# A two-layer GDN and FoX trunk: the opening in two column halves, kept PSUM banks, the last gates in other buffers, and other planned distances

## The chip, the cores and the metric

The kernel runs on one NeuronCore of a Trainium2 chip, in one launch. The metric is the device time of one execution in microseconds (us). The kernel before was timed three times: 1981.58 us in the median, 1981.22 to 1984.26. One further execution was profiled; spans and waits below come from it. In the profile PE is TensorE, PEld its weight loads, DVE is VectorE, ACT ScalarE, POOL GpSimd and SP SyncE, which issues nearly all DMA transfers.

## The reference

The trunk has two layers over 1024 tokens of width 1024 in float32, steered by one vector c:

```python
cond = jax.nn.silu(c)
for i in range(DEPTH):
    mod = cond @ ada_w[i] + ada_b[i]
    shift, scale, gate = jnp.split(mod[:, None, :], 3, axis=-1)
    h = rmsnorm(x, norm_w[i]) * (1 + scale) + shift
    y = gdn_mixer(...) if i % 2 == 0 else fox_mixer(...)
    x = x + gate * y
return rmsnorm(x, final_norm_w)
```

Layer 0 is a gated delta rule (GDN): h times the input projection gives q and k for 8 heads and v and z for 16 heads of 128, and two gates per v head (b and a). q, k and v pass through a causal convolution of width 4 and SiLU. In chunks of 64 tokens (the kernel takes 128) the rule is

```python
T = inverse of (I + L),  L = strictly lower part of (k*beta) k^T * decay
v_new = T @ (v*beta) - (T @ (k*beta*exp(g))) @ state
o     = (q*exp(g)) @ state + attn @ v_new
state = state * exp(g_last) + k_dec^T @ v_new
```

The output is normed per head, multiplied by silu(z) and projected by a 2048 x 1024 matrix. Layer 1 is attention with a forget gate (FoX), 16 heads of 64. The change concerns layer 0 and the way to layer 1 alone.

## The kernel before

**Stages.** Layer 0 works on two halves of 512 tokens (h = 0, 1), and in each on eight groups g: one q/k head with its two v heads. The opening (`start_norm`, L547) norms and transposes the first half of x, builds shift and scale (`scol`, `gcol`) from `ada_w`, modulates to `ht_h` and `ht_l` (each float32 value split into two parts) and projects the gates. `proj_all` (L801) then runs through 16 groups: k, q, two v tiles and two z tiles each. A tile is 8 k steps of `mm3`, three 128x128 by 128x512 matmuls (high by high, high by low, low by high), so 24 matmuls; 96 tiles make 2304 of them. Beside that flow run `prepk`, `invert_blocks`, `invert_merge` (the inverse T, by blocks, with a round trip through DRAM), `prepv` and `prep2` (transposes to token order, attention products), `chain` (the state recurrence) and `finish` (norm, gate, store of `og_d` and `ogl_d`). `out_proj_a` (L460) multiplies by the output matrix, half 0 with `ohi`, `olo` and half 1 with `yh`, `yl`, loaded back from `og_d` and `ogl_d`; the results go through POOL (L506) and are stored to `x_d` (L508) for layer 1.

**What sets the order.** A small planner in Python (`Flow`, L89) writes TensorE's program. Each stream is a generator with a priority; it issues matmuls and yields a number of nanoseconds before which it isn't to be taken up again. The planner's clock `flow.t` advances by a cost per matmul, so that a yield of 1700 means some eight wide matmuls of other streams in between. The `Y_*` constants are these distances. `bank`, `both` and `free` (L145 to L165) plan PSUM banks: a stream waits until a bank is free on the planner's clock. TensorE runs exactly this order. On the other engines and on SP a scheduler orders the instructions by its own model of time, and each engine takes them in order.

**Names.** In `chain` a step is: `ch` = k by state (L1000 or so), `xp`, `ch` = T by xp, `vn` and `ve`, `co` = attention by vn and `co` = k by `ve`, then the state update on VectorE (L1047 for a first step, L1049 otherwise), `yield Y_C2`, and the next step's `ch`, which needs the state. `Y_PV` stands in `prepv` (L950) between a group's projections and the transposes of q and v (`tr<-ident,vt`), which read the projections' results (`vt` L799). `LAT` is the planned latency of the round trip of `invert_blocks` (L1106); after it `invert_merge` takes two `su` and two `tr` banks at once (`both`) and runs small matmuls (`su<-tmat`). `Y_GA` stands ahead of the matmuls on the gates. `KPE` says for how many of the eight rows of k in the opening VectorE multiplies and adds ada_w by `cond`; the others and the sum go through narrow matmuls with one column (128x1) on TensorE. `zg` are the gates silu(z), in a ring of two (`ZG`); k and q have rings of four (`KQ`).

## Time and profile before

| what | before |
|---|---|
| median of 3 runs | 1981.58 us |
| the profiled execution | 1981.06 us |
| its span, first to last instruction | 1979.3 us |
| mean granted clock of TensorE | 0.966 |
| PE busy | 1838.8 us (93%) |
| DVE busy | 1334.9 us (67%) |
| ACT busy | 1030.6 us (52%) |
| DMA moved | 307.18 MB, 155 GB/s |
| opening, to the first wide projection matmul | 0 to 62.3 us |
| layer 0's projections and recurrence | 62.3 to 994.3 us |
| rest of layer 0's recurrence with half 0 of its output projection | 994.3 to 1119.6 us |
| half 1 of it, beginning of layer 1 | 1119.6 to 1215 us |
| layer 1 | 1215 to 1979.3 us |

The span is 1.8 us shorter than the execution's time. A granted clock of 1.00 is full speed, 0.50 half; in a table by stage it is the mean over the stretch. "Idle before, releaser" in a row of the profile is the time that the engine stood before it and what came last. The names in a row are those of the tiles without their numbers; a reused buffer keeps the name of its ring (`og`, `zg`, `k`, `q` hold ada_w or x in the opening).

### The profile page before, as it was taken

The page shows a single profiled execution, that of the slowest core. Times are in us where ns is not written, and L with a number is a line of the kernel's source. Part 1 is how long each engine was busy: PE and PEld are TensorE (multiplying, and loading weights), DVE is VectorE, ACT ScalarE, POOL GpSimd, SP SyncE. Part 2 cuts the span into 40 slices and gives each one's busy share as a digit, 9 for nine tenths or more (in the row PEclk, how much of TensorE's full clock was granted, in tenths as well). Part 3 has the DMA queues.
Part 4 walks back from the last instruction along what each step waited for, and adds up shares of the span by engine and source line. Part 5 has one row for each costly group of instructions (what it writes and reads, how often), then busy time and mean ns, then how long its engine had stood idle before and what let it go on. Part 6 is the DMA issues. An engine that isn't in the chain of part 4 may idle for free.

```text
span 1979.3 us, 35876 instructions
## 1 busy us (share of the span) xinstructions
PE 1838.8 (93%) x12892; PEld 1536.0 (78%) x12892; DVE 1334.9 (67%) x3321; ACT 1030.6 (52%) x2672; POOL 375.2 (19%) x402
## 2 busy tenths in 40 slices
PE   4989989999898999999999889999999999999898
PEld 4868777777786777787777667788988889889676
DVE  6577877888776777776655676456656656656764
ACT  4455656665554445555544444256556655655631
POOL 2010101111111010100010243332232232231322
PEclk6889999999998999999999999999999999999999
DMA  7477556766665564554389985021111120211523
GB/s 265 165 232 245 182 179 198 251 219 225 206 194 170 166 198 146 181 170 137 96 291 311 349 311 201 13 64 49 44 60 38 49 65 27 59 54 49 166 90 96
DMA packets 222874, 307.18 MB, mean 155 GB/s; under 512 B 100396, under 2 KB 136876, under 8 KB 222696
## 3 DMA queue, kind: packets, MB, share of 16 engines
q1 hardware_dynamic: 222696, 304.88, 47.2%
q8 instruction: 102, 1.67, 0.3%
q14 instruction: 76, 0.62, 0.1%
HBM read 223.15 MB, written 81.67 MB: 154 GB/s over the span
## 4 chain that ended last, share of the span: by engine, by line
PE 60%; DVE 15%; DMA 14%; ACT 4%; issue 3%; SPq 3%; POOL 2%; DVEq 0%; POOLq 0%; ACTq 0%
PE mm L132 38%; PE lg L132 5%; PE oT L132 3%; PE pt L136 3%; DMA nx<-in_ada_w_dram 3%; PE su L132 3%; PE tr L136 3%; PE ch L132 2%; DVE wlo L331 2%; DMA lb<-d 1%; PE co L132 1%; DMA lr<-lb 1%; DMA ohi<-og_d 1%; DVE cv_y L792 1%; DVE d L929 1%
## 5 line engine op out<-in xcount | busy, mean ns | idle before, releaser
L132 PE MATMUL mm<-ht_h,whi 128*128 128x512 f32 x768 | 346.2, 451 | 0.2 <-ACT cv_y L784 0.2
L132 PE MATMUL mm<-ht_l,whi 128*128 128x512 f32 x768 | 308.3, 401 | 0.9 <-POOL ht_l L331 0.8
L132 PE MATMUL mm<-ht_h,wlo 128*128 128x512 f32 x768 | 308.6, 402 | 0.0
L132 PE MATMUL mm<-whi,h_h 128*128 128x384 f32 x512 | 186.3, 364 | 0.9 <-DVE kn L1487 0.9
L132 PEld LDWEIGHTS mm<-ht_h,wlo 128*128 128x128 f32 x768 | 148.8, 194 | 34.5
L132 PE MATMUL mm<-whi,h_l 128*128 128x384 f32 x512 | 172.4, 337 | 0.0
L132 PEld LDWEIGHTS mm<-ht_h,whi 128*128 128x128 f32 x768 | 149.9, 195 | 28.6 <-issue 1.7
L132 PE MATMUL mm<-wlo,h_h 128*128 128x384 f32 x512 | 172.1, 336 | 0.0
L132 PEld LDWEIGHTS mm<-ht_l,whi 128*128 128x128 f32 x768 | 149.9, 195 | 26.6 <-POOL ht_l L331 2.0
L1638 DVE TENSOR_TENSOR ptl<-pt,pth 128x512 fp32r<-128x512 f32 x192 | 106.3, 555 | 91.5 <-ACT pth L1637 89.6
L1637 ACT CAST pth<-pt 128x512 fp32r<-128x512 f32 x192 | 91.1, 476 | 138.8 <-PE pt L136 138.0
L792 DVE SCALAR_TENSOR_TENSOR cv_y<-cv_t,conv_h,cv_y 128x512 f32<-128x512 f32 x192 | 143.1, 745 | 16.6 <-ACT cv_y L784 14.4
L331 DVE TENSOR_TENSOR wlo<-ht_h,whi 128x512 fp32r<-128x512 f32 x124 | 97.5, 826 | 47.0 <-ACT whi L328 45.4
L1602 ACT ACTIVATE lg<-lg,mx 128x896 f32<-128x896 f32 (+7 forms) x128 | 99.5, 777 | 53.1 <-DVE mx L1594 47.3
L1481 POOL TENSOR_TENSOR rs<-ss,mhalf 128x4 f32<-128x4 f32 x64 | 64.5, 1007 | 330.6 <-DVE ss L1479 326.2
L328 ACT CAST whi<-ht_h 128x512 fp32r<-128x512 f32 x124 | 70.7, 618 | 89.8 <-DMA ht_h<-in_wa_o_dram 40.1
L132 PE MATMUL mm<-h_h,whi 128*128 128x512 f32 x240 | 99.9, 416 | 0.7 <-DVE wlo L1737 0.3
L132 PEld LDWEIGHTS mm<-whi,h_h 128*128 128x128 f32 x512 | 97.3, 190 | 3.5 <-ACT v L1483 1.2
L132 PEld LDWEIGHTS mm<-wlo,h_h 128*128 128x128 f32 x512 | 96.8, 189 | 2.0
L136 PE MATMUL pt<-ident,lg 128*128 128x128 f32 (+1 forms) x584 | 95.6, 272 | 2.2 <-ACT lg L1602 2.2
L132 PEld LDWEIGHTS mm<-whi,h_l 128*128 128x128 f32 x512 | 96.1, 188 | 0.0
L132 PE MATMUL mm<-h_h,wlo 128*128 128x512 f32 x240 | 94.3, 393 | 0.0
(373 smaller groups left out, 4505.0 us busy)
## 6 DMA issues: line engine op xcount, KB each, us to landing
ht_h<-in_wa_o_dram SPq DMA_DIRECT2D x62, 512.0 KB, 5.6
wc<-whi SPq DMA_DIRECT2D x45, 512.0 KB, 4.3
wc<-wlo SPq DMA_DIRECT2D x45, 512.0 KB, 4.8
wlo<-wc SPq DMA_DIRECT2D x45, 512.0 KB, 4.4
whi<-wc SPq DMA_DIRECT2D x45, 512.0 KB, 3.9
wlo<-in_wa_c_dram SPq DMA_DIRECT2D x35, 512.0 KB, 4.2
nx<-in_ada_w_dram SPq DMA_DIRECT2D x64, 256.0 KB, 4.8
wraw<-in_wb_dram SPq DMA_DIRECT2D x56, 256.0 KB, 2.7
```

Source lines behind the costliest of these rows:

```text
L132: self.nc.tensor.matmul(out, lhsT, rhs, start=start, stop=stop)
L136: self.nc.tensor.transpose(out, src, ident)
L328: nc.scalar.copy(hi, src)
L331: (lo_eng or nc.gpsimd).tensor_tensor(lo, src, hi.bitcast(F32), op=ALU.subtract)
L792: nc.vector.scalar_tensor_tensor(y, raw[:, j : j + HALF], w[:, j : j + 1], y, op0=ALU.mult, op1=ALU.add)
L929: nc.vector.scalar_tensor_tensor(lm[:, u], mq[:, c * P : (c + 1) * P], wn[:, c, j : j + 1], t["d2"][:, u], op0=ALU.mult, op1=ALU.mult,)
L1481: nc.gpsimd.tensor_tensor(rs, ss, mhalf[:, 0:4], op=ALU.pow)
L1602: nc.scalar.activation(lg, lg, AF.Exp, scale=-1.0, bias=mx[:, hh : hh + 1], accum_out=sums[:, tt : tt + 1],)
L1637: nc.scalar.copy(ph_[:, cs], pp[:, cs])
L1638: nc.vector.tensor_tensor(pl_[:, cs], pp[:, cs], ph_[:, cs].bitcast(F32), op=ALU.subtract)
```

## The change

Four things.

1. **Opening.** `ada_w` comes in two column halves instead of shift and then scale: a load takes 512 columns of shift and the same 512 of scale. Of half 0 VectorE takes 7 of the 8 rows of k and TensorE one, of half 1 five and three (`KPE`). After half 0 the first four tiles of h are modulated, after half 1 the others. The gate projection becomes `mm3` with the 32 gate columns stationary and 512 tokens moving, and four transposes turn the result. Small parameters are loaded by ScalarE's queue rather than SP's. The x tiles 1 to 3 are issued on SP behind the eight loads of half 0.
2. **Kept banks.** While a merge waits in `both` for its four banks, no other stream takes one of them.
3. **Last gates.** The gates of group 7 of each half lie in a k and a q buffer, not in the `zg` ring, with other conditions on when they may be written; k of groups 8 to 10 may be written one group later.
4. **Distances.** `Y_PV` 6500 to 8000; `Y_C2` 1700 to 2500 up to group 4 of half 1, 1700 after that (`Y_C4`); `Y_GA` 14000 to 9000 for half 0; `LAT` 40000 to 33000 for the first two groups.

The diff, without the constants' first lines and the code that only moves:

```diff
-Y_PV = 6500
+Y_PV = 8000
-Y_C2 = 1700
+Y_C2 = 2500
+Y_C4 = 1700
-KPE = 7
+KPE = (7, 5)
+Y_GA0 = 9000
+LAT0 = 33000
...
     def bank(self, key, bufs, alloc):
         ring = self.rings.setdefault(key, [0, [0.0] * bufs])
+        while key in self.kept:
+            yield 150
...
     def both(self, keys):
+        self.kept = keys
         while any(v > self.t for k in keys for v in self.rings[k][1]):
             yield 100
+        self.kept = ()
...
+            def ada_load(c0):
+                acc = at([P, 2, HALF], "d2", 3)
+                ws = []
                 for k in range(KT):
-                    w = at([P, D], *wtag())
-                    nc.sync.dma_start(w, ada_w[0, k * P : (k + 1) * P, n * D : n * D + D])
+                    w = at([P, 2, HALF], *wtag())
+                    nc.sync.dma_start(
+                        w, ada_w[0, k * P : (k + 1) * P, 0 : 2 * D].rearrange("p (n f) -> p n f", n=2)[
+                            :, :, c0 * HALF : c0 * HALF + HALF
+                        ],
+                    )
...
-                    elif k < KPE:
+                    elif k < KPE[c0]:
...
-                for t in range(CPH):
-                    mm(
-                        pc[:, t * 32 : t * 32 + 32], xk[:, t * P : (t + 1) * P], wba[:, k],
-                        start=k == 0 and t == 0, stop=k == KT - 1 and t == CPH - 1,
-                    )
                 nc.vector.tensor_tensor(ht_l[:, k], xk, ht_h[:, k].bitcast(F32), op=ALU.subtract)
+                mm3(pc[0:32], wbh[:, k], wbl[:, k], ht_h[:, k], ht_l[:, k], k == 0, k == KT - 1)
+
+            ws = ada_load(0)
+            split(wbh, wbl, wba, lo_eng=nc.vector)
+            yield from ada_sum(0, ws)
+            for k in range(4):
+                modulate(k)
+            ws = ada_load(1)
+            yield from ada_sum(1, ws)
+            for k in range(4, KT):
+                modulate(k)
...
-            yield Y_GA
+            yield (Y_GA0, Y_GA)[h]
...
-                yield from hold(lambda: done["core"] >= i + 1 - KQ)
+                yield from hold(lambda: done["core"] >= i + 1 - KQ + (NG <= i < NG + 3))
...
+                    if m % NG == NG - 1:
+                        yield from hold(lambda: done["core"] >= m + 2 - KQ)
+                        zg = [at([P, HALF], "k", KQ), at([P, HALF], "q", KQ)]
...
-                yield Y_C2
+                yield Y_C2 if (h, g) < (1, 5) else Y_C4
...
-            t["end"] = max(flow.t + Y_R2, t0 + LAT)
+            t["end"] = max(flow.t + Y_R2, t0 + (LAT if t["h"] or t["g"] > 1 else LAT0))
```

The added lines move the code down: L132 (`mm`) is L136 afterwards, L136 (`tr_`) is L140.

**TensorE's opening.** First the order before; `tr<-ident` are transposes of x, `mm<-ones,d` and `mm<-cond,...` the narrow matmuls on ada_w, `tr<-wba` the gate projection.

```order
L136 MATMUL tr<-ident,vtok 128x128 x24
L136 MATMUL tr<-ident,d_240 128x128 x8
L132 MATMUL mm<-ones,d_270 128x1 x8
L132 MATMUL mm<-cond,og 128x1 x8
L132 MATMUL mm<-ones,d_328 128x1 x8
L132 MATMUL mm<-cond,zg 128x1 x8
L132 MATMUL tr<-wba,k 128x32 x12
L132 MATMUL tr<-wba,q 128x32 x8
L132 MATMUL tr<-wba,ktok 128x32 x12
```

And after; `su` has taken the place of `mm`, `vn` holds the split gate weights, `cv_t` the projected gates.

```order
L140 MATMUL tr<-ident,vtok 128x128 x24
L140 MATMUL tr<-ident,d_240 128x128 x8
L136 MATMUL su<-cond,d_300 128x1 x8
L136 MATMUL su<-ones,d_278 128x1 x8
L136 MATMUL tr<-ht_h,vn 32x512
...
L136 MATMUL su<-cond,gb 128x1 x8
L136 MATMUL su<-cond,vt 128x1 x8
L136 MATMUL su<-cond,d_368 128x1 x8
L136 MATMUL su<-ones,d_348 128x1 x8
L136 MATMUL tr<-ht_h,vn 32x512
...
L140 MATMUL tr<-ident,cv_t 128x32 x4
L136 MATMUL mm<-ht_h,whi 128x512
```

The 32 narrow matmuls before, in two places of 16, have become 16 and 32; the gate projection stands between and behind them as 24 wide matmuls, and 32 narrow ones now stand behind the first 12 of these.

**A state step on TensorE** in the first group, from the `co` that completes the state to the `ch` that reads it, before:

```order
L132 MATMUL co<-ve,ktok 128x256
L132 MATMUL mm<-ht_h,whi 128x512
L132 MATMUL mm<-ht_l,whi 128x512
L132 MATMUL mm<-ht_h,wlo 128x512
L136 MATMUL tr<-ident,nx 128x128 x4
L132 MATMUL su<-k 128x128 x4
L132 MATMUL ch<-state_141,k 128x256
```

And after:

```order
L136 MATMUL co<-ve,ktok 128x256
L136 MATMUL su<-rmat_131,pq 64x64 x8
L136 MATMUL mm<-ht_h,whi 128x512
L136 MATMUL mm<-ht_l,whi 128x512
L136 MATMUL mm<-ht_h,wlo 128x512
L136 MATMUL mm<-ht_h,whi 128x512
L136 MATMUL mm<-ht_l,whi 128x512
L136 MATMUL mm<-ht_h,wlo 128x512
L136 MATMUL su<-k 128x128 x4
L136 MATMUL ch<-state_141,k 128x256
```

Between `co<-ve` and `ch<-state` stood three wide matmuls and two groups of four narrow ones, and now stand six wide ones and eight and four small ones. In later groups the typical step goes from nine wide matmuls to twelve; from group 5 of half 1 on nothing changes.

**SP between the two halves of the output projection**, with what each issue waits for beside the ring, before. `x_d<-ht_l` are the last results of half 0, `yh` and `yl` the first operands of half 1, `ht_h<-in_wa_o` output weights.

```order
L446 DMA yh<-og_d 128x2x256 [waits DMAHW2_49]
L1384 DMA fb<-in_f_bias_dram 128x16 [waits DMAHW3_49]
L446 DMA yl<-ogl_d 128x2x256 [waits DMAHW4_49,Pool_49]
L446 DMA yh<-og_d 128x2x256 [waits DMAHW5_49]
L446 DMA yl<-ogl_d 128x2x256 [waits DMAHW6_49]
L446 DMA yh<-og_d 128x2x256 [waits DMAHW7_49]
L446 DMA yl<-ogl_d 128x2x256 [waits DMAHW0_49]
L508 DMA x_d<-ht_l 128x1024 [waits DMAHW1_49,Pool_49]
L418 DMA ht_h<-in_wa_o_dram 128x1024 [waits DMAHW2_49,DVE_49]
L446 DMA yh<-og_d 128x2x256 [waits DMAHW3_49]
L508 DMA x_d<-ht_l 128x1024 [waits DMAHW4_49,Pool_49]
```

And after, where `v` and `kn` (left out) are loads for layer 1:

```order
L516 DMA x_d<-ht_l 128x1024 [waits DMAHW4_49,Pool_49]
L426 DMA ht_h<-in_wa_o_dram 128x1024 [waits DMAHW5_49,DVE_49]
L1133 DMA ogl_d<-ogl 128x512 [waits DMAHW6_49,DVE_49]
L516 DMA x_d<-ht_l 128x1024 [waits DMAHW7_49,Pool_49]
L426 DMA ht_h<-in_wa_o_dram 128x1024 [waits DMAHW0_49,DVE_49]
L426 DMA ht_h<-in_wa_o_dram 128x1024 [waits DMAHW1_49,DVE_49]
...
L1363 DMA v<-x_d 128x1024 [waits DMAHW6_49]
L1418 DMA qk_c<-in_qkn_dram 128x2 [waits DMAHW7_49]
L454 DMA yh<-og_d 128x2x256 [waits DMAHW0_49]
L1421 DMA fb<-in_f_bias_dram 128x16 [waits DMAHW1_49]
L454 DMA yl<-ogl_d 128x2x256 [waits DMAHW2_49]
```

The two stores to `x_d`, which wait for POOL, stood behind three pairs of `yh` and `yl`; now they stand ahead of the first `yh`. TensorE's order is the same in both from the middle of half 1 on, and VectorE's in its last 1030 rows.

More of the change, by code (lines that the diff above doesn't have):

```diff
@@ L581, in start_norm, with ada_sum, modulate @@
                         )
-                    for s, c, on in ((acc, ones[:, 0:1], k == KPE), (w, cond[:, k : k + 1], k >= KPE)):
-                        for j in range(KT if on else 0):
-                            mm(
-                                ps[:, j : j + 1], s[:, j * P : (j + 1) * P], c,
-                                start=s is acc and j == 0, stop=s is w and k == KT - 1 and j == KT - 1,
-                            )
-                if n == 0:
-                    nc.sync.dma_start(wba, wa_ba)
-                    nc.sync.dma_start(dt_b, a_dt.broadcast_to([P, 16]))
-                    nc.sync.dma_start(neg_a, a_log.broadcast_to([P, 16]))
-                    nc.sync.dma_start(bcol, ada_bc)
-                    nc.sync.dma_start(norm_c, norm_col)
-                    wload()
-                    wload()
-                nc.vector.tensor_tensor((scol, gcol)[n][0], ps[:, 0:KT], bcol[:, n], op=ALU.add)
+                    else:
+                        ws.append((w, cond[:, k : k + 1]))
+                return ws + [(acc, ones[:, 0:1])]
+            def ada_sum(c0, ws):
+                ps = yield from pst("su", 2)
+                for i, (w, c) in enumerate(ws):
+                    for j in range(KT):
+                        n, jj = divmod(j, 4)
+                        mm(
+                            ps[:, j : j + 1], w[:, n, jj * P : (jj + 1) * P], c,
+                            start=i == 0 and j == 0, stop=i == len(ws) - 1 and j == KT - 1,
+                        )
+                cs = slice(4 * c0, 4 * c0 + 4)
+                nc.vector.tensor_tensor(gcol[0][:, cs], ps[:, 4:8], bcol[:, 1, cs], op=ALU.add)
+                nc.vector.scalar_tensor_tensor(
+                    gcol[0][:, cs], gcol[0][:, cs], 1.0, norm_c[:, 0, cs], op0=ALU.add, op1=ALU.mult
+                )
+                nc.vector.tensor_tensor(scol[0][:, cs], ps[:, 0:4], bcol[:, 0, cs], op=ALU.add)
                 flow.free(ps, R_AD)
-            nc.vector.scalar_tensor_tensor(
-                gcol[0], gcol[0], 1.0, norm_c[:, 0], op0=ALU.add, op1=ALU.mult
-            )
             pc = yield from pst("tr", 2)
-            for k in range(KT):
+            def modulate(k):
                 xk = xsT[k]
@@ L609, in start_norm @@
                     nc.vector.tensor_scalar(xk, xk, sc, sh, op0=ALU.mult, op1=ALU.add)
-                for t in range(CPH):
-                    mm(
-                        pc[:, t * 32 : t * 32 + 32], xk[:, t * P : (t + 1) * P], wba[:, k],
-                        start=k == 0 and t == 0, stop=k == KT - 1 and t == CPH - 1,
-                    )
-                nc.vector.tensor_tensor(ht_l[:, k], xk, ht_h[:, k].bitcast(F32), op=ALU.subtract)
-            flow.add(gates(0, gts[0], pc[:, 0 : CPH * 32].rearrange("p (c n) -> p c n", n=32), pc), 1, HC)
-            nc.sync.dma_start(conv_h, conv_col)
+                nc.vector.tensor_tensor(ht_l[:, k], xk, ht_h[:, k].bitcast(F32), op=ALU.subtract)
+                mm3(pc[0:32], wbh[:, k], wbl[:, k], ht_h[:, k], ht_l[:, k], k == 0, k == KT - 1)
[8 more added lines that the diff above has]
+                modulate(k)
+            rows = at([P, HALF + 3], "cv_t", 2)[0:32, 0:HALF]
+            nc.scalar.copy(rows, pc[0:32])
+            flow.free(pc, R_AD)
+            wload()
+            half(2)
+            pg = yield from pst("tr", 2)
+            for t in range(CPH):
+                tr_(pg[:, t * 32 : t * 32 + 32], rows[:, t * P : (t + 1) * P], ident[0:32, 0:32])
+            flow.add(gates(0, gts[0], pg[:, 0 : CPH * 32].rearrange("p (c n) -> p c n", n=32), pg), 1, HC)
             nc.vector.tensor_scalar(conv_h, conv_h, 0.5, None, op0=ALU.mult)
-            nc.sync.dma_start(nw_h, a_nw)
             nc.vector.tensor_scalar(nw_h, nw_h, 0.5, None, op0=ALU.mult)
@@ L831, in proj_all @@
                 for m in z_after(i):
[L832 to L833 removed]
+                    if m % NG == NG - 1:
+                        yield from hold(lambda: done["core"] >= m + 2 - KQ)
+                        zg = [at([P, HALF], "k", KQ), at([P, HALF], "q", KQ)]
+                    else:
+                        yield from hold(lambda: done["chain"] >= m + 1 - ZG)
+                        zv = at([P, 2, HALF], "zg", ZG)
+                        zg = [zv[:, j] for j in range(2)]
                     for j in range(2):
```

24 lines of the change are left out of this document (12 added, 12 removed).

## The prediction

> **What bounds the kernel now.** I read the stages first, then TensorE's waits in the stage of the projections, then single waits and what VectorE did during them, then the opening and the place between the two halves of the output projection. A table by stage gives microseconds, busy time (and records) of PE, PEld, DVE, ACT and POOL, the granted clock, the DMA share and GB/s:
>
> ```profile
> core 0: us, PE busy (x) PEld busy (x) DVE busy (x) ACT busy (x) POOL busy (x), PEclk, DMA share, GB/s
> ...
> 20.60:62.40 41.80, 27.97 (x129) 27.67 (x129) 20.66 (x31) 11.27 (x17) 0.00 (x0) 0.50 0.39 151
> 62.40:67.40 5.00, 5.00 (x13) 3.94 (x13) 4.31 (x18) 0.62 (x3) 0.00 (x0) 0.50 0.00 0
> ...
> 105.00:994.30 889.30, 828.59 (x7438) 674.52 (x7439) 666.60 (x1801) 490.48 (x1480) 99.87 (x149) 0.97 0.59 187
> 994.30:1119.60 125.30, 114.79 (x568) 88.91 (x566) 69.85 (x123) 53.29 (x126) 12.96 (x8) 0.97 0.96 319
> 1119.60:1215.00 95.40, 84.01 (x360) 64.49 (x359) 75.63 (x134) 47.39 (x91) 42.32 (x27) 0.96 0.88 312
> ...
> ```
>
> TensorE is busy most of the time once the opening is over. The long stage from 105.0 to 994.3 us holds two losses: 889.3 - 828.6 = 60.7 us idle, and a mean clock of 0.97, so about 0.03 x 889 = 27 us (22 to 31 by the rounding) lost to half clock. From the middle of the second half of the output projection on, TensorE keeps its order, so that the sum ends there. The idle time in that stage, by what ended it (total, times, longest):
>
> ```profile
> PE ch L132 <- DVE state L1049: 19.0, 10, 4.1
> PE tr L136 <- ACT vtok L964: 8.2, 3, 5.9
> PE ch L132 <- DVE state L1047: 7.8, 3, 3.6
> PE tr L136 <- DVE vt L799: 5.8, 2, 3.5
> PE su L132 <- DVE tmat L1148: 4.8, 4, 2.6
> ...
> PE tr L136 <- DVE k L799: 3.0, 1, 3.0
> ```
>
> The waits for the state are 26.8 us in 13 cases, those for v and k 17.0 in 6. One of the state waits, on TensorE and then on VectorE:
>
> ```profile
> 374.77 1.19 PE L132 MATMUL ch<-state,k 128*128 128x256 f32 x2 [3.61 <-DVE state L1049]
> ...
> 372.69 0.75 DVE L277 SCALAR_TENSOR_TENSOR nh<-nx,cond,nh 128x512 f32<-128x512 f32 x1 [1.16 <-DMA nx<-in_ada_w_dram]
> 374.02 0.60 DVE L1049 SCALAR_TENSOR_TENSOR state<-state,g_ex,co 128x128 f32<-128x128 f32 x2
> ```
>
> TensorE had used up its fillers at 374.77 - 3.61 = 371.2 and stood until the state came; VectorE had stood 1.16 us on a load of ada_w with the state update queued behind it. After such waits the clock falls. Windows that begin 1.3, 0.7 and 0 us after the ends of waits of 2.28, 1.65 and 3.61 us:
>
> ```profile
> 134.49 0.55 PE L136 MATMUL tr<-ident,vt 128*128 128x128 f32 x3 [2.28 <-DVE vt L799]
> 909.90 0.66 PE L136 MATMUL tr<-ident,vt 128*128 128x128 f32 x4 [1.65 <-ACT vtok L964]
> ...
> 135.80:139.20 3.40, 3.40 (x11) 2.74 (x10) 1.85 (x10) 0.95 (x3) 0.00 (x0) 0.50 0.92 304
> 910.60:914.00 3.40, 3.40 (x9) 2.64 (x8) 2.69 (x14) 1.47 (x6) 1.77 (x2) 0.50 0.08 30
> ...
> 374.80:378.00 3.20, 3.20 (x70) 2.24 (x71) 2.98 (x10) 1.50 (x6) 0.00 (x0) 0.50 0.72 267
> ```
>
> **A, the opening: -2.5 us (-11 to +1.5).** TensorE and ScalarE (x tiles being squared) before:
>
> ```profile
> 5.10 1.06 ACT L310 ACTIVATE nx<-vtok 128x1024 f32<-128x1024 f32 x1 [2.48 <-DMA vtok<-in_x_dram]
> 9.00 1.06 ACT L310 ACTIVATE nx<-d 128x1024 f32<-128x1024 f32 x1
> 14.81 1.79 PE L136 MATMUL tr<-ident,d 128*128 128x128 f32 x8
> 36.32 3.58 PE L132 MATMUL mm<-ones,d 128*128 128x1 f32 x16 [8.68 <-DVE d L579]
> ...
> 43.34 0.17 DVE L596 TENSOR_TENSOR gcol<-mm,bcol 128x8 f32<-128x8 f32 x1 [5.23 <-PE mm L132]
> 44.65 0.55 DVE L609 TENSOR_SCALAR k<-k,gcol,scol 128x512 f32<-128x512 f32 x1 [0.94 <-ACT ht_h L605]
> 46.06 0.55 DVE L609 TENSOR_SCALAR k<-k,gcol,scol 128x512 f32<-128x512 f32 x1
> 62.29 0.77 PE L132 MATMUL mm<-ht_h,whi 128*128 128x512 f32 x1
> ```
>
> The four x tiles of 512 KB are squared as they arrive, 1.3 us apart ((9.00 - 5.10) / 3). In the new order eight ada_w loads of that size stand between the first x tile and the other three, so the last one comes at 5.1 + 11 x 1.3 = 19.4 instead of 9.0. Its transposes end 7.6 later, as before (14.81 + 1.79 - 9.00): 27.0. Behind them on TensorE stand 16 narrow matmuls; eight cost 3.58 us at half clock (two records each), so 7.1. Then 0.5 for the columns, modulation of four tiles with their 12 wide matmuls (1.41 us a tile by 44.65 and 46.06, plus an end: 6.3), 32 narrow ones (14.3), 0.5, four more tiles (6.5), one copy and four transposes (1.6). The sum is 63.8. One row, from the stage of the projections, has narrow matmuls at full clock (busy time, mean ns, idle before):
>
> ```profile
> L132 PE MATMUL mm<-ones,nh 128*128 128x1 f32 x32 | 3.9, 243 | 0.0
> ```
>
> That is 3.9 for 16 matmuls; with it for all 48 the sum is 63.8 - 48 x 0.2 = 54 (rounded). The projections began at 62.3. I take 61, since the 32 follow 12 wide ones that may wake the clock; it is nearer the half-clock end because the old opening ran at 0.50 throughout from 20.6: -1.3. The projections' first 5.0 us were at 0.50 as well, which lost 2.5; the new wide matmuls under the modulation may warm the clock for half of it: -1.2. The old narrow gate projections are gone, their wide successors lie under the modulation. The parameter loads on ACT's queue lie under the DMA time and count nothing; if ACT were late by one, all of it moves by about 0.4.
>
> **B, state waits: -10 (-5 to -16).** Typical steps have 12 wide fillers behind the last co, not 9. Two wide matmuls in a row, the last of half 0:
>
> ```profile
> 1119.10 0.39 PE L132 MATMUL mm<-wlo,ohi 128*128 128x512 f32 x1
> 1119.33 0.39 PE L132 MATMUL mm<-whi,olo 128*128 128x512 f32 x1
> ```
>
> They start 0.23 us apart; three are 0.7, and the planner's distance grows by 0.8 (2500 against 1700 ns). 13 waits x 0.8 = 10.4, less what waits shorter than that lack: 10. The fillers aren't extra work, they come from elsewhere. What is late next is the update itself wherever VectorE is further behind than 0.8 us.
>
> **C, waits for v and k: -8 (-3 to -12).** The planned 8000 against 6500 ns shifts the transposes by 1.5 us: 1.5 of the 3.51, all of the 1.65, 1.5 of the 2.28, the 3.0 of k (by the order some 5 us more work stands ahead of it, an estimate at 0.23 us a wide matmul), 0.4 for the rest. The 5.9 of the first v stays: ScalarE there has a second group's exponentials ahead.
>
> **D, half clock: -8 (0 to -14).** About a third of the 27 us. At half clock a 3.4 us window does 1.7 us of work less; five windows or so, 8 us, follow waits that B and C remove. By the Trainium skill, page TensorE: Matmul & The Clock Gate, section Part 1: The HAM clock gate, the clock halves after at least one idle window of about 3.4 us, and its abstract rule is no gap above that. The trace does not agree as far as that goes: windows at 0.50 follow waits of 1.65 and 2.28.
>
> **E, new waits: +4 (0 to +14).** For the first two groups the planner's latency of the inverse's round trip falls from 40 to 33 us, and gates of the first half come after 9 us, not 14. VectorE stands on that trip already, so that nothing says that 7 us of slack is there twice:
>
> ```profile
> DVE xtmp L1121 <- DMA lr<-lb: 25.5, 12, 4.0
> DVE tmat L1148 <- DMA rmat<-rb: 23.3, 14, 5.1
> DVE nh L277 <- DMA nx<-in_ada_w_dram: 17.5, 15, 2.1
> ```
>
> I take the worst existing merge wait class (4.8 in all) once more, less one. The kept banks and the last gates in k and q buffers I cost at nothing: other projection tiles cover a held k; if that cover is gone a k wait like the 3.0 above comes back.
>
> **F, between the halves: +8 (+2 to +13).** SP, TensorE and POOL before:
>
> ```profile
> 1117.45 0.38 SPq L446 DMA_DIRECT2D yh<-og_d  x1
> 1124.73 0.48 SPq L508 DMA_DIRECT2D x_d<-ht_l  x1
> 1127.95 0.97 SPq L418 DMA_DIRECT2D ht_h<-in_wa_o_dram  x1
> ...
> 1122.83 0.77 PE L132 MATMUL mm<-whi,yh 128*128 128x512 f32 x1 [3.11 <-DMA yh<-og_d]
> 1119.84 2.94 POOL L506 TENSOR_TENSOR ht_l<-ht_l,wlo 128x512 f32<-128x512 f32 x2 [25.26 <-DVE wlo L503]
> ```
>
> The first yh load was issued 1.9 us before the last matmul of half 0 began (1119.33) and landed 5.4 us later (1122.83 - 1117.45). Now it stands on SP behind both x_d stores, which wait for POOL's adds (to 1122.8, 3.5 us after that matmul; the second store went out at 1124.73), then three weight loads that wait for VectorE's splits, and six more issues of about 0.5. Its issue is at the earliest 3.5 + 9 issues x 0.4 = 7 after that matmul; by the old time of the third weight load (1127.95) and the six issues it is at 8.6 + 3 = 11.6. With 4 to 5.4 for the flight TensorE idles 11 to 17 us, not 3.1. Behind yh on SP wait its partner yl and four loads of x. This part of the program is limited by transfers (share 0.96 and 0.88), so some of it is given back as shorter waits later; hence 8.
>
> **Sum.** -2.5 - 10 - 8 - 8 + 4 + 8 = -16.5 on the profiled execution of 1981.06, which lies 0.5 under the median of 1981.58: 1964.6, and on the median's footing 1965. Its own range is 1953 to 1979.
>
> **Rivals.**
> 1. VectorE is the bound of the state steps (slower). It is busy 666.6 of 889.3 us, takes its work in order, and in the quoted case lay idle on a load with the update behind it. If TensorE's longer distances only run ahead of an engine that is late by as much more, B, C and D give nothing: -2.5 + 4 + 8 = +9.5, 1991. It decides once B, C and D together give less than 9.5. Against it: 25% of VectorE is free, and most updates are late by single operations. Chance 0.17.
> 2. The clock stays up. If the falls need an idle run near the length of a window and the short waits left behind reach none, D takes 20 of the 27: sum -28.5, 1953. For it: the falls come after waits that shrink. Against it: those after 1.65 and 2.28 us. The rule of the idle window from the Trainium skill, page TensorE: Matmul & The Clock Gate, Part 1, would give this time. Chance 0.15.
> 3. The order changes but not what ends the waits: fillers moved in one place are missing in the next, and opening, B, C, D only pay for E and F: 1981. Chance 0.06.
>
> **Numbers.** The forecast has 0.62, with under a tenth of it above -4 us. A difference under 0.2% (4 us) can't be told from none: faster means under 1977.6, slower over 1985.5. Faster 0.62 x 0.9 + 0.15 = 0.71, same 0.06 + 0.06 = 0.12, slower 0.17. The range from 1948 to 1988 takes in rival 2 and leaves out the worse half of rival 1.
>
> **What would show it.** A: first wide projection matmul at about 61, narrow ones at 0.45. B: the two state rows at about 17 instead of 26.8. C: the k row gone, v rows near 9. D: clock 0.98 from 105 to the end of the projections. E: merge rows (su on tmat) at 9 instead of 4.8. F: one yh wait above 9 us. It is wrong if the state rows don't shrink or the yh wait stays near 3.

## The result, and the profile after

The changed kernel takes 1957.6 us in the median of four runs (1950.17 to 1963.85), the one before 1982.92 (1981.22 to 1988.28). The ratio is 0.9873, with a 95% interval of 0.9851 to 0.9895: 25 us faster. The profiled execution of the changed kernel took 1963.85, the slowest of its four, against 1981.06: there the difference is 17.2, and the comparison of the traces below accounts for these 17.2; the other 8 of the medians are in no trace.

The stages of the changed kernel, cut at events: the first wide projection matmul, the end of the last one, the end of half 0 of the output projection, and the first matmul of layer 1.

```profile
core 0: us, PE busy (x) PEld busy (x) DVE busy (x) ACT busy (x) POOL busy (x), PEclk, DMA share, GB/s
0.00:63.90 63.90, 37.15 (x157) 27.80 (x157) 31.16 (x53) 24.82 (x63) 8.52 (x26) 0.87 0.56 205
63.90:958.50 894.60, 850.21 (x7436) 693.18 (x7436) 689.11 (x1854) 506.29 (x1509) 101.13 (x163) 0.98 0.62 196
958.50:1089.70 131.20, 117.33 (x751) 91.98 (x749) 73.03 (x136) 59.37 (x145) 11.78 (x8) 1.00 0.90 301
1089.70:1211.40 121.70, 99.83 (x434) 80.29 (x434) 80.74 (x147) 52.04 (x99) 41.29 (x28) 0.90 0.79 275
1211.40:1962.10 750.70, 720.90 (x4117) 629.53 (x4115) 452.57 (x1136) 388.98 (x858) 203.07 (x178) 0.99 0.19 62
```

The same events in the kernel before:

```profile
62.30:994.00 931.70, 867.72 (x7618) 706.85 (x7619) 695.13 (x1867) 511.49 (x1528) 105.40 (x162) 0.96 0.60 189
994.00:1119.70 125.70, 115.19 (x569) 89.16 (x567) 69.95 (x123) 53.56 (x127) 12.96 (x8) 0.97 0.95 318
1119.70:1232.30 112.60, 101.21 (x434) 78.43 (x434) 83.60 (x146) 52.14 (x99) 43.49 (x28) 0.97 0.79 282
1232.30:1979.30 747.00, 719.07 (x4117) 628.04 (x4115) 452.70 (x1136) 389.22 (x858) 203.08 (x178) 0.99 0.19 62
```

The opening is 1.6 us longer, the projections 37.1 shorter, the rest of half 0 5.5 longer (it holds some 180 more small records, work that moved there), the way to layer 1 9.1 longer, layer 1 3.7 longer. The 0.87 of the opening counts the time before the first clock record, at 43.5 us, as full speed, though the narrow matmuls there took the times of half speed (below). In the projections TensorE stands 44.4 us instead of 64.0, and the granted clock is 0.98 instead of 0.96. Summed over windows of 5 us from 65 us on, (1 - clock) x time is 18.3 us instead of 32.0. Layer 1 has the same order on TensorE; in all fourteen profiled executions of this study it took 747.0 to 752.2 us, and the kernel before is at the lower end, so I put the 3.7 down to the execution, not to the change.

What TensorE waits for in the projections afterwards (total, times, longest):

```profile
PE tr L140 <- ACT vtok L1001: 11.1, 4, 5.9
PE tr L140 <- ACT rmat L1209: 5.5, 3, 3.0
PE su L136 <- DVE tmat L1214: 4.8, 5, 2.7
PE ch L136 <- DVE state L1086: 4.0, 6, 1.2
...
PE ch L136 <- DVE state L1084: 2.0, 1, 2.0
...
PE su L136 <- DVE tmat L1239: 1.8, 3, 1.0
PE tr L140 <- DVE vt L831: 1.7, 1, 1.7
```

The state rows are 6.0 us instead of 26.8, in 7 cases instead of 13. The k row is gone. The rows for v are 12.8 and 0.6 more in a row not shown (17.0 with k before); the first wait of 5.9 has stayed. A row for `rmat` in the merges is new.

The opening on TensorE:

```profile
26.50 2.19 PE L140 MATMUL tr<-ident,d 128*128 128x128 f32 x8
28.48 3.41 PE L136 MATMUL su<-cond,d 128*128 128x1 f32 x16
31.75 3.55 PE L136 MATMUL su<-ones,d 128*128 128x1 f32 x16
36.66 0.63 PE L136 MATMUL tr<-ht_h,vn 128*32 128x512 f32 x1 [1.36 <-ACT ht_h L625]
...
43.59 1.84 PE L136 MATMUL su<-cond,gb 128*128 128x1 f32 x16
45.28 2.07 PE L136 MATMUL su<-cond,vt 128*128 128x1 f32 x16
47.22 3.55 PE L136 MATMUL su<-cond,d 128*128 128x1 f32 x16
50.63 3.55 PE L136 MATMUL su<-ones,d 128*128 128x1 f32 x16
55.48 0.64 PE L136 MATMUL tr<-ht_h,vn 128*32 128x512 f32 x1 [1.30 <-ACT ht_h L625]
...
63.87 0.80 PE L136 MATMUL mm<-ht_h,whi 128*128 128x512 f32 x1
```

Eight narrow matmuls cost 3.4 to 3.6 us, then, by their starts, 1.7 and 1.9 behind the 12 wide ones (43.59, 45.28), then 3.5 again. Between the halves, SP and TensorE:

```profile
1091.18 0.32 SPq L516 DMA_DIRECT2D x_d<-ht_l  x1
...
1094.41 0.38 SPq L516 DMA_DIRECT2D x_d<-ht_l  x1
...
1101.29 0.38 SPq L454 DMA_DIRECT2D yh<-og_d  x1
```

```profile
1109.00 0.76 PE L136 MATMUL mm<-whi,yh 128*128 128x512 f32 x1 [19.25 <-DMA yh<-og_d]
```

The last matmul of half 0 began at 1089.36. The first yh load went out 11.9 us later, behind both stores, and TensorE stood 19.25 us instead of 3.11.

### The profile page after: what moved, and what is told of

It reads as the page before. It is cut to its first block, busy times and chain, and to the rows that moved or that the text cites. A ratio compares the mean times of both kernels' runs of the same rounds, so it can differ in the third digit from the quotient of the medians.

```text
span 1962.1 us, 35871 instructions
## 1 busy us (share of the span) xinstructions
PE 1825.4 (93%) x12888; PEld 1522.8 (78%) x12888; DVE 1326.6 (68%) x3323; ACT 1031.5 (53%) x2674; POOL 365.8 (19%) x402
## 4 chain that ended last, share of the span: by engine, by line
PE 68%; DMA 12%; DVE 12%; ACT 4%; issue 2%; SPq 1%; POOL 1%; ACTq 0%; DVEq 0%; POOLq 0%
PE mm L136 42%; PE lg L136 6%; PE su L136 4%; PE pt L140 4%; PE oT L136 3%; PE tr L140 3%; PE ch L136 3%; DMA nx<-in_ada_w_dram 2%; PE co L136 2%; DVE wlo L339 2%; DMA ht_h<-in_wa_o_dram 1%; DMA ohi<-og_d 1%; DMA rmat<-rb 1%; DVE cv_y L824 1%; ACT whi L336 1%
## 5 line engine op out<-in xcount | busy, mean ns | idle before, releaser
L136 PE MATMUL mm<-ht_h,whi 128*128 128x512 f32 x768 | 342.7, 446 | 0.5 <-DVE nh L312 0.5
L136 PE MATMUL mm<-ht_h,wlo 128*128 128x512 f32 x768 | 305.6, 398 | 0.0
L136 PE MATMUL mm<-ht_l,whi 128*128 128x512 f32 x768 | 304.9, 397 | 0.2 <-POOL ht_l L339 0.2
L136 PE MATMUL mm<-whi,h_h 128*128 128x384 f32 x512 | 186.5, 364 | 0.9 <-DVE kn L1524 0.9
L136 PEld LDWEIGHTS mm<-ht_h,wlo 128*128 128x128 f32 x768 | 146.5, 191 | 33.6
L136 PE MATMUL mm<-whi,h_l 128*128 128x384 f32 x512 | 172.5, 337 | 0.0
L136 PE MATMUL mm<-wlo,h_h 128*128 128x384 f32 x512 | 172.4, 337 | 0.0
L136 PEld LDWEIGHTS mm<-ht_h,whi 128*128 128x128 f32 x768 | 147.6, 192 | 28.7 <-issue 2.1
L136 PEld LDWEIGHTS mm<-ht_l,whi 128*128 128x128 f32 x768 | 147.9, 193 | 24.4 <-POOL ht_l L339 0.6
L339 DVE TENSOR_TENSOR wlo<-ht_h,whi 128x512 fp32r<-128x512 f32 x124 | 93.2, 792 | 56.0 <-ACT whi L336 46.7
L136 PE MATMUL mm<-h_h,whi 128*128 128x512 f32 x240 | 100.5, 419 | 0.7 <-DVE wlo L1774 0.3
L136 PEld LDWEIGHTS mm<-whi,h_h 128*128 128x128 f32 x512 | 97.5, 190 | 3.5 <-ACT v L1520 1.2
L140 PE MATMUL pt<-ident,lg 128*128 128x128 f32 (+1 forms) x584 | 96.1, 274 | 3.5 <-ACT lg L1639 3.5
L136 PEld LDWEIGHTS mm<-wlo,h_h 128*128 128x128 f32 x512 | 96.9, 189 | 2.0
L136 PEld LDWEIGHTS mm<-whi,h_l 128*128 128x128 f32 x512 | 96.2, 188 | 0.0
L136 PE MATMUL mm<-h_h,wlo 128*128 128x512 f32 x240 | 94.9, 395 | 0.0
```

The source lines that it names most:

```text
L136: self.nc.tensor.matmul(out, lhsT, rhs, start=start, stop=stop)
L140: self.nc.tensor.transpose(out, src, ident)
L339: (lo_eng or nc.gpsimd).tensor_tensor(lo, src, hi.bitcast(F32), op=ALU.subtract)
```

## The experiments

Theory 1 was that of the prediction: each distance cures its own wait, and the parts add up. The rivals were that another part or VectorE decides. After the first eight runs theory 1 had fallen, and theory 2 took its place: the parts work only together. Ratios are against the kernel before, on the same chip, with 95% intervals. Losses and gains in percent below are differences of these ratios. The traces are of one execution each, which can lie far from its median: the change's is 6 us above it, u_val's 10 above, c1_xd_pool_yh's 9 below.

| kernel | median us | ratio | interval |
|---|---|---|---|
| the change | 1957.6 | 0.9873 | 0.9851 to 0.9895 |
| u_state | 1970.7 | 0.9955 | 0.9928 to 0.9982 |
| u_val | 1982.5 | 1.0007 | 0.9986 to 1.0029 |
| u_open | 1954.5 | 0.9862 | 0.9826 to 0.9898 |
| u_z | 1979.3 | 0.9991 | 0.9969 to 1.0013 |
| u_lat | 1981.8 | 0.9997 | 0.9982 to 1.0011 |
| u_kept | 1992.1 | 1.0050 | 1.0024 to 1.0077 |
| b_state | 2021.0 | 1.0192 | 1.0175 to 1.0209 |
| b_z | 1987.4 | 1.0032 | 1.0012 to 1.0051 |
| b_z_state | 2001.9 | 1.0102 | 1.0067 to 1.0138 |
| c1_xd_pool_yh | 1967.4 | 0.9914 | 0.9884 to 0.9944 |
| x_first | 1951.8 | 0.9840 | 0.9816 to 0.9863 |
| x_first_c3 | 1954.8 | 0.9862 | 0.9829 to 0.9894 |

To see where a kernel loses time, I cut the projections of each trace into 16 equal stretches of work, by the start of every 48th of the 768 matmuls `mm<-ht_h,whi`. A stretch is about one group. The four that differ most, the sum of all 16, TensorE's idle time and (1 - clock) x time in them, in us:

| kernel | 4 | 8 | 10 | 16 | all | idle | clock |
|---|---|---|---|---|---|---|---|
| before | 74.1 | 62.4 | 58.8 | 59.3 | 931.3 | 64.0 | 32.0 |
| the change | 61.0 | 58.2 | 55.1 | 52.2 | 894.2 | 44.4 | 18.3 |
| u_state | 62.7 | 63.9 | 57.7 | 50.1 | 897.0 | 46.4 | 20.4 |
| u_val | 71.8 | 56.6 | 59.2 | 52.8 | 913.6 | 50.6 | 32.5 |
| u_open | 62.9 | 58.8 | 56.0 | 52.2 | 889.6 | 38.9 | 17.3 |
| u_z | 62.3 | 76.8 | 46.9 | 66.1 | 914.5 | 48.2 | 32.4 |
| u_lat | 76.2 | 56.6 | 55.9 | 52.3 | 907.4 | 52.9 | 23.9 |
| u_kept | 73.3 | 71.4 | 69.8 | 51.1 | 922.9 | 66.3 | 30.3 |
| b_state | 73.6 | 82.5 | 58.5 | 68.8 | 947.6 | 70.4 | 37.4 |
| b_z | 74.4 | 60.1 | 55.0 | 50.6 | 910.6 | 55.1 | 22.1 |
| b_z_state | 74.3 | 59.2 | 61.7 | 60.3 | 941.6 | 74.2 | 37.2 |

**u_state**, the changed kernel with one edit:

```diff
-                yield Y_C2 if (h, g) < (1, 5) else Y_C4
+                yield Y_C4
```

> The changed kernel with the distance behind the state back at 1700 ns everywhere, everything else as changed. Theory 1 (each distance cures its own wait): the waits for the state between 62 us and the end of the projections come back, from 6.0 us in the changed kernel to 20 to 27, with some 3 to 8 us of half clock; no wide matmul is left between the last transposes of og and the end of half 0 (12 in the changed kernel), so the wait for yh stays at 19 or grows by up to 3. Time 20 to 33 us over the changed kernel, 1978 to 1990. Rival (the state waits went because of other parts, the kept banks or the z gates in k and q): state rows stay under 10 us and the time within 6 us of the changed kernel.

The state row in the projections came back, to 16.1 us, the wait for yh grew to 25.9, and the kernel lost 0.8% (16 us) against the change:

```profile
PE ch L136 <- DVE state L1086: 16.1, 13, 3.9
```

The rival is out: the distance does cure this wait. But the row is smaller than expected, and the whole projection stage only 2.8 us longer than the changed kernel's; the way from half 0 to layer 1 is 6.3 us longer (128.0 against 121.7). The two profiled executions lie only 3.7 us apart, so most of the 16 us of the medians is not placed.

**u_val**:

```diff
-Y_PV = 8000
+Y_PV = 6500
```

> The changed kernel with the distance ahead of the transposes of q and v back at 6500 ns. Theory 1: vt and vtok rows go from 13.4 us together in the changed kernel to 17 to 21, other rows stay, the yh wait stays at 19 or a little more (no wide matmul behind the last og transposes): 4 to 12 us over the changed kernel, 1962 to 1970. Rival (the v waits end on VectorE and ScalarE, which are no earlier for it): the rows stay within 2 us, and the time within 4 us.

A miss. The rows for v did not grow (only the k row came back, with 3.0 us), yet the time went back to that of the kernel before, 27 us over the change. The projections took 913.6 us: stretch 4 lost 10.8 and stretch 6 5.8 (68.3 against 62.5), TensorE waited 7.3 us for `nh` in four places, the clock term is 32.5 instead of 18.3. None of this is what the edited distance stands in front of. The trace is of the slowest of its ten runs, so that the sizes are upper ones.

**u_lat**:

```diff
-            t["end"] = max(flow.t + Y_R2, t0 + (LAT if t["h"] or t["g"] > 1 else LAT0))
+            t["end"] = max(flow.t + Y_R2, t0 + LAT)
...
-            yield (Y_GA0, Y_GA)[h]
+            yield Y_GA
```

> The changed kernel with the planned round trip of the first two groups back at 40 us and the gates of half 0 back at 14 us. If the shorter distances cost merge waits (my term of +4): this kernel's rows for su on tmat and tr on rmat before 200 us fall from what the changed kernel has there, and it is 2 to 6 us faster. If they bring time (an earlier merge, an earlier chain): the chain of half 0 ends later, and it is 3 to 10 slower.

Slower by 1.2% (25 us), so that the two shorter distances together bring time; the run does not separate them. The first merge begins at 154.8 instead of 143.6. Stretch 4 alone is 15.2 us longer (76.2 against 61.0), the projections as a whole 13.2. The expected fall of the merge rows before 200 us had no room: TensorE waited there 0.7 us for tmat in the changed kernel, 0.2 here, and never for rmat.

**u_kept**:

```diff
-        self.kept = keys
```

> The changed kernel without the kept banks alone. I costed this part at nothing (-1.5 to +1.5). If each part only works with the others: 15 to 25 us slower than the changed kernel, as without the z gates, near 1980. If it is worth nothing by itself: within 5 us of it, but the yh wait at 24 to 27 since by the order no wide matmul lies behind the last og transposes: 1960 to 1966.

Slower by 1.8% (35 us) than the change: by the medians, the part that I costed at nothing is worth more than any other here. Stretches 4, 8 and 10 are 12 to 15 us longer each. In stretch 10 a merge stands on VectorE for 11 us, and VectorE in turn stands 3.75 us on a load of the inverse's round trip (`rmat<-rb`). The row of the waits in the projections, and the rows of that one wait on TensorE and then VectorE:

```profile
PE su L136 <- DVE tmat L1184: 11.3, 2, 11.1
```

```profile
614.36 0.29 PE L136 MATMUL su<-tmat,d 16*32 16x16 f32 x2 [11.09 <-DVE tmat L1184]
613.87 0.43 DVE L1184 STREAM_TRANSPOSE tmat<-rmat 32x256 f32<-32x256 f32 x1 [3.75 <-DMA rmat<-rb]
```

**u_z**:

```diff
-                    if m % NG == NG - 1:
+                    if False:
...
-                yield from hold(lambda: done["core"] >= i + 1 - KQ + (NG <= i < NG + 3))
+                yield from hold(lambda: done["core"] >= i + 1 - KQ)
```

> The changed kernel with the gates of group 7 in the ring again and the hold of groups 8 to 10 as before. By the order 66 wide matmuls then lie between the last transposes of og and the end of half 0, not 12 (0.23 us each, so 12 us more time for the round trip of og through DRAM). If the yh wait hangs on that distance: it falls from 19.3 to 3 to 8 us; against that, waits for k or z of at most 5 us in the projections: 5 to 14 faster than the changed kernel, 1944 to 1952. If it hangs on SP's order of stores alone (they stand ahead of yh or not), the wait is below 4 only when yh stands ahead of x_d, and otherwise stays above 14.

The wait for yh did go (0.15 us), with 66 wide matmuls behind the last og transposes. But the kernel was 23 us slower than the change, not faster: the ends of both halves, stretches 8 and 16, took 18.6 and 13.9 us more. These are the groups whose gates the edit puts back into the ring. In this order yh also went out ahead of both x_d stores (1100.66 against 1115.05), so that the run does not tell the distance of the og transposes from SP's order.

**b_state**, the kernel before with the one distance (in its constants 2500, and 1700 from group 5 of half 1 on):

```diff
-                yield Y_C2
+                yield Y_C2 if (h, g) < (1, 5) else 1700
```

> The kernel before with one edit: the distance behind the state 2500 ns instead of 1700 up to group 4 of half 1. Theory 1 (the distance alone cures the state waits): state rows from 26.8 us to under 10, half clock by 5 to 10 us less; 90 wide matmuls behind the last og transposes, so that the yh wait stays at 3 to 5: 17 to 27 us faster than before, ratio 0.986 to 0.992. Rival (VectorE is late by as much more, or the fillers are missing elsewhere): state rows above 18, ratio above 0.996.

Slower by 1.9% (38 us). The state rows halved, from 26.8 to 13.4, and other waits came up in their place, in the projections:

```profile
PE ch L132 <- DVE state L1049: 9.2, 7, 2.7
PE ch L132 <- DVE xp L1004: 8.0, 6, 2.6
...
PE co L132 <- ACT vn L1020: 5.3, 5, 1.7
PE tr L136 <- DVE k L799: 5.0, 1, 5.0
PE co L132 <- DVE ve L1024: 4.5, 4, 3.0
PE ch L132 <- DVE state L1047: 4.2, 2, 2.4
```

Stretch 8 took 82.5 us against 62.4, stretch 16 68.8 against 59.3. This ends theory 1: the wait that was aimed at shrank, and the kernel lost. Hence theory 2: with longer steps the recurrence is later, the gates of the last group wait for it in the ring of two at the end of each half, and only the change's other buffers take that away.

**b_z and b_z_state**, the kernel before with the part on the gates alone, and with that and b_state's distance:

```diff
+                    if m % NG == NG - 1:
+                        yield from hold(lambda: done["core"] >= m + 2 - KQ)
+                        zg = [at([P, HALF], "k", KQ), at([P, HALF], "q", KQ)]
```

> The kernel before with one part of the change: the gates of group 7 in a k and a q buffer, with its holds. Theory 2 (the parts work together: longer distances make the recurrence later, and in the ring of two the last gates then wait for it at the end of each half): alone, without the longer distance, this saves only what the kernel before loses there; the state waits stay at 20 to 27 us, the last og transposes come 10 us nearer to the end of half 0 by the order (0 wide matmuls behind them, not 42), so the yh wait grows to 20 to 27. Time 1970 to 1990. Rival (the z gates alone are the gain): under 1965.

> The kernel before with both: the last gates in k and q buffers and 2500 ns behind the state; the old opening, no kept banks, other distances as before. With the distance alone it was at 2021 us. Theory 2: state waits stay under 12 us as with the distance alone, and the two stretches in which that kernel lost time, groups 7 and 15, are 14 to 25 us and 10 to 15 us shorter; the yh wait is 17 to 21. Time 1960 to 1985, so 35 to 60 under the distance alone. Rival (the parts are independent): the distance's loss of 38 us stays, 2005 to 2025 less what the z gates alone bring.

b_z was 0.3% slower than before: its projections are 21 us shorter, and the rest of half 0 (6.6 us longer) and the way to layer 1 (13.6 longer, with a wait for yh of 24.1) take that back. In b_z_state stretch 8 fell from 82.5 to 59.2 and stretch 16 from 68.8 to 60.3 against b_state: where theory 2 puts the loss, most of it went. But the state rows, expected under 12, stood at 20.3 (15.4 and 4.9): in this order the longer distance hardly cured its own wait. The forecast of the total missed: 2001.9, 20 over the kernel before, since stretch 4 stayed at 74.3 and stretches 12 and 13 grew (62.6 and 65.6 against 58.6 and 58.0 in b_state). So the gates' buffers account for the ends of the halves and not for the rest.

**u_open**, the changed kernel with the whole old opening (and KPE = 7):

```diff
-            ws = ada_load(0)
...
+            for n in range(2):
+                ps = banks[n]
```

> The changed kernel with the old opening (shift, then scale; gate projection in 32-column matmuls; KPE 7). The traces have the first wide projection matmul at 62.3 us before and at 63.9 after. If the opening stands by itself, the changed kernel loses 1 to 2 us there, and this kernel is 1 to 2 us faster than it, 1955 to 1957 (not to be told from it). Rival (the new opening pays behind the start, by a warm clock and by group 0's order): this kernel is 4 or more slower, over 1961.

1954.5 us, not to be told from the change. The first wide projection matmul was at 62.3. The new opening neither brings nor costs anything that can be measured.

**x_first**:

```diff
-                nc.sync.dma_start(xt, x[t * P : (t + 1) * P, :])
+                with tc.high_priority(offset=3000):
+                    nc.sync.dma_start(xt, x[t * P : (t + 1) * P, :])
```

> The changed kernel with all four x tiles loaded ahead of ada_w, as before the change. The last x transposes end at about 17 us instead of 28.5, the 16 narrow matmuls of half 0 start when VectorE's seven rows are done, at about 21 to 23 instead of 28.5: the first wide projection matmul 5 to 8 us earlier, 56 to 59 us, and the time 4 to 8 us lower, 1950 to 1954. Rival (half 1 of ada_w, loads and five rows on VectorE, ends last): under 3 us.

The four x tiles are loaded first again, and the projections begin at 57.75 instead of 63.87, as expected:

```profile
16.15 1.97 PE L140 MATMUL tr<-ident,d 128*128 128x128 f32 x8
21.71 3.57 PE L136 MATMUL su<-cond,d 128*128 128x1 f32 x16 [3.60 <-DMA d<-in_ada_w_dram]
25.15 3.55 PE L136 MATMUL su<-ones,d 128*128 128x1 f32 x16
30.26 0.64 PE L136 MATMUL tr<-ht_h,vn 128*32 128x512 f32 x1 [1.56 <-ACT ht_h L626]
```

The narrow matmuls now wait for their own load (3.6 us) rather than for x. The ratio of 0.9840 is the best of the study, though its interval overlaps the change's.

**c1_xd_pool_yh**, two edits at the boundary:

```diff
-                    nc.sync.dma_start(x1_d[h * CPH + t], xs[:, t])
+                    (nc.sync if h else nc.gpsimd).dma_start(x1_d[h * CPH + t], xs[:, t])
...
+                with tc.high_priority(offset=1000):
                     nc.sync.dma_start(v.bitcast(F32), d[k : k + 2, :, tok : tok + w].rearrange("k p t -> p k t"))
```

> The changed kernel with SP relieved at the boundary: the x_d stores of half 0 go out through POOL's queue, and yh and yl are put ahead of the loads for layer 1 on SP. Theory (the yh wait is SP's order): yh issues about 7 us earlier, after three weight loads that wait for VectorE; the wait falls from 19.3 to 8 to 13: 5 to 10 faster than the changed kernel, 1947 to 1953. Rival (yh waits for the place of buffers that the last og stores free, and for DRAM traffic): yh starts at most 2 us earlier, time within 3 us.

yh went out 7.0 us after the end of half 0 (1089.30 against 1082.3), not 11.5 (1101.29 against 1089.75), right behind the last of the three weight loads, and the wait fell to 13.8, a little over the 8 to 13 expected. The time did not fall: 0.9914. The stretch of the wait and the rest of half 1 in this kernel:

```profile
1082.30:1096.00 13.70, 0.00 (x0) 0.01 (x1) 6.58 (x9) 1.14 (x2) 4.03 (x4) 0.66 0.77 271
1096.00:1205.60 109.60, 101.60 (x432) 80.48 (x433) 78.14 (x138) 50.75 (x97) 39.26 (x26) 0.95 0.77 271
```

Together 123.3 us against 121.7 in the changed kernel: 5.5 won at the wait, 7.2 lost behind it (109.6 against 102.4). There TensorE waits 5.0 us for VectorE's weight splits, which it did not in the changed kernel; before the longest of them, 3.75 us, VectorE has 4.0 us of layer 1's work ahead of the split. The median is 10 us over the change's, 8 by the ratios, and the intervals overlap a little; the trace, of an execution 5 us under the change's, doesn't explain that.

**x_first_c3**:

```diff
-                yield Y_C2 if (h, g) < (1, 5) else Y_C4
+                yield Y_C2 if (h, g) < (1, 3) else Y_C4
```

> The version with all x tiles loaded first, and the long distance behind the state only up to group 2 of half 1 instead of group 4. By the order 36 wide matmuls then lie behind the last og transposes, not 12. If the yh wait is the time of the round trip from these transposes (22.6 us in the changed kernel) less what TensorE still has to do: 24 x 0.23 = 5.5 us shorter, 19.3 to 13 to 14.5, with 1 to 3 us more state waits in half 1: 1946 to 1950, 2 to 5 under the version with x first alone. Rival: the projections end later by as much, no change.

No change against x_first. The first yh was in time, but the weights came 3.5 us late and yl 7.9: 11.3 us idle instead of 19.3; the stretch from the end of half 0 to layer 1 went from 119.1 to 116.9, and the rest of half 0 grew from 130.5 to 134.8.

The boundary over all kernels. Wide matmuls between the last og transposes and the end of half 0 (by the order), time from these transposes to the first yh matmul, TensorE's wait there (in b_state and the first of x_first_c3 for weights), and the time from the end of half 0 to layer 1, in us:

| kernel | matmuls | og to yh | wait | to layer 1 |
|---|---|---|---|---|
| before | 42 | 17.8 | 3.1 | 112.5 |
| the change | 12 | 22.6 | 19.3 | 121.7 |
| u_state | 0 | 26.9 | 25.9 | 128.0 |
| u_val | 0 | 26.8 | 25.7 | 129.7 |
| u_open | 12 | 22.5 | 19.1 | 120.9 |
| u_lat | 0 | 24.5 | 23.9 | 124.1 |
| u_kept | 0 | 26.3 | 25.3 | 127.0 |
| u_z | 66 | 30.5 | 0.1 | 118.2 |
| b_state | 90 | 36.4 | 1.6 | 119.1 |
| b_z | 0 | 24.7 | 24.1 | 126.1 |
| b_z_state | 12 | 23.3 | 19.8 | 121.6 |
| c1_xd_pool_yh | 12 | 17.1 | 13.8 | 123.4 |
| x_first | 12 | 22.6 | 19.3 | 119.1 |
| x_first_c3 | 36 | 17.4 | 3.5 and 7.9 | 116.9 |

The wait for yh is the time from og to yh less the work that TensorE has left meanwhile. What sets that time differs, and it is not always the way of og through DRAM. In this program at most eight transfers of SP are under way: an issue goes out only when the eighth transfer ahead of it has landed: the fourteen traces have that landing for 4211 issues, and none of them starts earlier. What the first yh load waited for on SP (total, times, longest), in the changed kernel and in u_state:

```profile
SPq L454 <- DMA ht_h<-in_wa_o_dram: 0.5, 1, 0.5
```

```profile
SPq L454 <- DMA og_d<-ogh: 0.3, 1, 0.3
```

In the changed kernel the eighth transfer ahead is a weight load, issued at 1095.20 when VectorE's split allowed it and landed at 1101.28; the last store to og_d had landed at 1091.32, ten us before yh went out. In u_state, u_val and u_kept the eighth is that store itself (landed at 1109.02 in u_state, yh out at 1109.04).

Half 1 behind an early start takes 109 to 118 us, behind a late one 100 to 103. Against the kernel before, between a quarter and three fifths of the added wait is given back (7 of 16 us in the change). I take it that this is because transfers go on meanwhile: in c1 the DMA share is 0.77 during the wait and 0.77 behind it.

## Why the prediction was right, point by point

The time was forecast at 1965 and came out at 1957.6, faster as forecast and inside the range; on the profiled executions -16.5 was forecast and -17.2 measured. That closeness is in part luck: by the medians the gain is 25, and 1957.6 lies nearer to the 1953 of rival 2 than to 1965. The terms, by the traces:

| term | forecast | measured | how |
|---|---|---|---|
| A opening | -2.5 | +1.6 | first wide projection matmul 62.3 to 63.9 |
| B state waits | -10 | -20.8 | rows 26.8 to 6.0 |
| C waits for v and k | -8 | -3.6 | 17.0 to 13.4 |
| D half clock | -8 | -13.7 | 32.0 to 18.3 in the projections |
| E merges and first groups | +4 | +4.0 | rows on tmat and rmat, 8.1 to 12.1 |
| F between the halves | +8 | +9.1 | 112.6 to 121.7 |

The measured terms add up to -23.4. What brings them to -17.2 is 5.5 in the rest of half 0 and 3.7 in layer 1, for which the forecast had no term, and -3.0 in the projections outside these rows. A and C came out 4.1 and 4.4 worse than forecast, B and D 10.8 and 5.7 better.

**A** failed on two sizes. The x transposes ended at 28.5 rather than 27.0, and each modulation took 8.1 and 8.3 us (35.5 to 43.6, 54.4 to 62.7), where I had put 6.3 and 6.5: its matmuls wait for VectorE's `ht_l`, and weight splits stand in between. The narrow matmuls were right, 6.8 and 10.6, between the two bounds for the second. No clock warmth was carried into the projections: they ran at full speed from 67.4, as before. That the place of the x loads costs some 6 us, x_first shows.

**B** had the right mechanism (u_state brings the row back) and too small a size: a wait that 0.8 us would only shorten did not come back elsewhere in this order. The step that failed is another, the one that says the terms add. "The fillers aren't extra work, they come from elsewhere" was in the text without a price; b_state, the distance alone, pays 38 us for it. So the rival in which VectorE decides was wrong in its mechanism, as VectorE has the same work in both (695 and 689 us) and the state still came earlier, but the warning in the third, that fillers moved in one place are missing in the next, was nearer to what happens when a part is taken alone.

**C** was right for k and half wrong for v: vt fell from 5.8 to 1.7 and vtok rose from 8.2 to 11.7. u_val shows that the distance is worth far more than the rows in front of which it stands, by a way that I can't name beyond the stretches in which the time goes.

**D** was right in direction and too small: the measured 13.7 lies between the 8 of the forecast and the 20 of rival 2, and 18.3 us at half clock remain. **E** has the right number by luck. Its sign, 4.8 to 9 in the rows of su on tmat, did not come (4.8 in the main row before and after); what grew is tr on rmat, and all but 0.7 of the 12.1 lies behind 200 us, where the first two groups' merges are past. u_lat shows that the shorter round trip and the earlier gates together are a gain of 25 us and not a cost.

**F** had the place and the net price right (9.1 against 8), with a wait of 19.25 over the forecast 11 to 17. Its mechanism shows in the trace: behind the x_d stores stand three weight loads that wait for VectorE (the last at 1096.41) and six more issues, and yh went out at 11.9 us, where the later of my two sums had 11.6. Too small was the flight, 7.6 us (1101.29 to 1108.87) against 4 to 5.4. c1 took away only 5.5 of the wait, since the weight loads still stood ahead of yh. What I had not seen is that the wait also grows when the last og transposes stand nearer to the end of half 0, to 25.9 in u_state.

The **kept banks**, costed at nothing because other tiles cover a held bank, were worth 35 us within the change. The cover argument looked at what the held streams lose, and not at the merge: without the hold one merge stood on VectorE for 11 us, 3.75 of them on the inverse's round trip. The 12 and 13 us that stretches 4 and 8 lose are not placed.

**What stays open.** Four parts (kept banks, the distance ahead of the v transposes, the shorter round trip with the earlier gates, the gates' buffers with their holds) each bring back 23 to 35 us when they alone are undone, though the whole change gains 25. Stretch 4 shows it: 71.8 to 76.2 us in every kernel in which kept banks, the 8000 ns or the shorter round trip is missing, 61 to 63 in the others. That each is needed beside the others is shown; alone, on the kernel before, only the gates' buffers and the distance behind the state were tried, and neither gained. Another reading is open too: the constants were found together, and any other order of this planner may be some 20 us worse. x_first_c3, which moves one distance for two groups and costs nothing measurable, is the only run that speaks against it. By which bank or which tile one hangs on the other, no run here separates, and the rest of u_val's and c1's losses is not placed either.

## What to carry to other kernels

In a program whose order is written by a planner, the waits of a profile tell where time goes, but not what a distance is worth: a constant that halves its own wait can lengthen others and lose in total. Price such a change as a whole by the order it gives (what stands between producer and consumer at the costly places, ends of phases above all), and never sum one-wait gains; when a set of constants was found together, undo them one at a time before keeping or dropping any. A wait on a transfer at a phase boundary is worth less than its length where other transfers that the next phase needs go on during it.
